# A two-layer decoder trunk: loading x from ScalarE's queue beside the weights, and a fixed order for the first three row tiles

## The chip, the cores and the metric

One core of a Trainium2 chip runs the whole program in one launch. The metric is device time in microseconds, the median of a few timed executions. The engines are TensorE (PE; its weight loads are listed as PEld), VectorE (DVE), ScalarE (ACT), GpSimd (POOL) and SyncE (SP, which here only issues DMAs). ScalarE can issue DMAs too; in the kernel before it issues none.

## The reference, cut to what matters

```python
def reference(x, ...):
    for l in range(DEPTH):                       # 2 layers
        h = _rmsnorm(x, pre_mix_norm[l])
        h = _hybrid_mixer(h, cos, sin, w_in[l], ...)   # proj = h @ w_in, then two kinds of mixing, then @ w_out
        x = x + _rmsnorm(h, post_mix_norm[l])
        h = _rmsnorm(x, pre_ffn_norm[l])
        h = _conv_glu_ffn(h, ffn_up[l], ...)
        x = x + _rmsnorm(h, post_ffn_norm[l])

def _rmsnorm(x, w):
    return (x * lax.rsqrt(jnp.mean(x * x, axis=-1, keepdims=True) + NORM_EPS)) * w
```

x is 512 positions by 1024 features, all in float32. The place of the change is the very first part: x times its gains, times the first columns of `w_in` (the keys of the DeltaNet heads) and times the eight small columns for `b` and `a` (the gates of these heads). The factor of the norm of each position (`rs` in the kernel) is multiplied in after the matmul.

## The kernel before, in words

**Three matmuls for one.** Each float32 operand is split into a high part in the matmul's own format and the rest: weights into `whi` and `wlo`, x times its gain into the two halves of `hx`. A product of a 128x128 piece of weights and a 128x512 piece of x is then a group of three matmuls: high by high, high by low, low by high (`mm3`, `mmk`). ScalarE writes the high part (`act`, L147), VectorE or GpSimd the low part (`tt`, L151; for x `stt`, L165), so a low part waits for its high part, and both for the landing of what they split.

**Row tiles.** x lies transposed: eight contraction tiles of 128 features by 512 positions, two to a tile `xt[0]` to `xt[3]`. A row tile is 128 columns of `w_in`: one unit of weights `raw`, 128x1024, for eight groups of three matmuls into one PSUM tile. The first three row tiles go to the three PSUM tiles `pss`, the later ones to `psg`. `was` are the split columns for `b` and `a`: 16 matmuls of 16 rows into a `psg`.

**The loads.** All DMAs go out on SP, in the order in which the program writes them: weight 0, the gains `vv`, x rows 0 and 1, weight 1, the three other pairs of x, `wa`, `rc`; then `loader` writes one load for every weight buffer that comes free. There are two `raw` buffers and four pairs of `whi` and `wlo` (HL).

**The order of the work.** The kernel's order is written by a planner in the program (`_Sched`): jobs are generators with priorities, a clock `sc.t` that adds up assumed costs, and flags with due times. The order in which jobs call an operation is the order of the instructions on its engine. `splitter` splits the weights in order, for the low part on VectorE or GpSimd, whichever the planner thinks free. `scale_split` splits an x tile; `square_sum` adds up x squared, with ScalarE squaring and GpSimd adding into `acc2`. `lead` multiplies whatever the planner takes for ready, row tile 0 first, then the `was` rows, then row tiles 1 and 2.

**What comes next.** From `acc2` four small matmuls, a step on VectorE (`rt`), a power on GpSimd and four more matmuls make `rs`, which ScalarE copies from PSUM. With it VectorE takes the row tiles out of PSUM (`A`), then works on the gates (`dn_...`), the convolution of the keys (`kT`) and the decays (`edec`). TensorE works on with further row tiles between them, in a fixed order in which rows that wait for VectorE stand.

**The warm-up.** Ahead of all this, five matmuls on a constant (`pso<-mhalf`) run while the loads are under way; each counts as two in the profile.

Of the kernel before, what the change touches and what calls it, by code (L numbers as in the profile page):

```python
# [10 lines left out]
F32 = mybir.dt.float32  # L11
# [7 lines left out]
P = 128  # L19
# [94 lines left out]
def kernel(ctx: ExitStack, tc: tile.TileContext, xT, w_ab, w_cm, w_tm, w_o, w_up, w_dn,  # L114
# [111 lines left out]
    for l in range(DEPTH):  # L226
# [10 lines left out]
        wseq += [(w_dn[l, m][:, 1024 * i:min(1024 * (i + 1), DFF)], min(1024, DFF - 1024 * i))  # L237
                 for m in range(KD) for i in range(3)]
        home[len(wseq) - 1] = ("xu", None)
    RAW, HL = 2, 4  # L240
    wraw, wunit = {}, {}
    wst = {"take": 0}

    def load(u, at):
        src, cols = wseq[u]
        raw = wp.tile([P, 1024], F32, tag="raw", bufs=RAW, name="raw")
        sync.dma_start(raw[:, :cols], src)
        wraw[u] = raw
        sc.set(("raw", u), at)

    def loader():
        sc.slots["raw"] = []
        for u in range(RAW, len(wseq)):
            yield from sc.get("raw", RAW)
            load(u, max(sc.t + 3.2, 13.4) if u == RAW else sc.t + 3.2)
            if u == RAW:
                sync.dma_start(cc, cst)

    def splitter():
        for u, (src, cols) in enumerate(wseq):  # L260
            yield from sc.wait(("raw", u))
            if u in home:
                tag, flag = home[u]
                if flag is not None:
                    yield from sc.wait(flag)
                if tag == "xu":
                    pair = xp.tile([P, 2, 768], F32R, tag="xu", name="wxu")
                else:
                    pair = sp.tile([P, 2, 1024], F32R, tag=tag, name="whome")
                hi, lo = pair[:, 0], pair[:, 1]  # L270
            else:
                yield from sc.get("wu", HL)
# [23 lines left out]
    def free(n=1, unit=None):  # L296
        for _ in range(n):
            if unit not in home:
                sc.put("wu", sc.t)
# [19 lines left out]
    def load_vec(l):  # L319
        v = cp.tile([P, V_W], F32, tag="vv", bufs=1, name="vv")  # L320
        sync.dma_start(v, vec[l])
        return v
# [15 lines left out]
        tt(was[:, :, 8:16], wa, was[:, :, 0:8].bitcast(F32), ALU.subtract, after=r)  # L338
        return was

    load(0, 4.0)
    vv = load_vec(0)
    for j in range(2):
        sync.dma_start(xt[0][:, j], xT[:, j])
    load(1, 7.3)
    for j in range(1, 4):
        sync.dma_start(xt[j], xT[:, 2 * j:2 * j + 2])
    wa0 = load_ab(0)
    rc = load_row(0)
    sc.set(("vec", 0))  # L350
# [27 lines left out]
    def scale_split(key, m, seg, hx, gain, acc2, after):  # L378

        t0, t1 = seg  # L380
        x = xs(m)[:, t0:t1]
        hi = hx[m][:, 0, t0:t1]
        r = act(hi, x, AF.Identity, scale=gain, after=after)
        if key != "in":
            sc.spawn(square_sum(key, m, seg, acc2), 0)
        yield r
        r = stt(hx[m][:, 1, t0:t1], x, gain, hi.bitcast(F32), ALU.mult, ALU.subtract, after=r)
        sc.set(("hx", key, m, t0), r)
        if key == "in":
            yield from sc.idle(("act",), 6.0)  # L390
            yield from square_sum(key, m, seg, acc2)

    def square_sum(key, m, seg, acc2):
        t0, t1 = seg
        x = xs(m)[:, t0:t1]
        if key != "in":
            yield from sc.wait(("rows", key, t0))
        if m == 0:
            r = act(acc2[:, t0:t1], x, AF.Square)
        else:  # L400
            sq = yield from wget("sq")
            r = act(sq[:, t0:t1], x, AF.Square)
            yield r
            yield from sc.wait(("sq", key, 0, t0))
            r = tt(acc2[:, t0:t1], acc2[:, t0:t1], sq[:, t0:t1], ALU.add, eng="pool", after=r)
            sc.put("sq", r)
        sc.set(("sq", key, m, t0), r)
# [245 lines left out]

    def mixer(l, key, hx, acc2, rs, segs):
        rhs = hl(hx)
        was = wab[l]
        pab = yield from pget("g")
        pss = []
        for _ in range(3):
# [4 lines left out]
        def ab_rows(kt, seg, first, last):  # L664
            t0, t1 = seg
            for j in range(2):
                mm(pab[0:16, t0:t1], was[:, kt], rhs(kt)[j][:, t0:t1], first and j == 0, last and j == 1)

        rt = kp.tile([P, 4], F32, tag="rt", bufs=1, name="rt")
        for seg in segs:  # L670
            yield from lead(key, pss, us, rhs, seg, seg is segs[-1], ab_rows)
            sc.spawn(pre_rstd(key, acc2, seg, rs, rt), 0)
        if l == 0:
            xd = xT
# [731 lines left out]
    def trunk():  # L1406
        nonlocal vv, rc
        key = "in"
        yield from sc.get("acc2", 1)
        acc2 = work("acc2")  # L1410
        yield from sc.get("rs", 1)
        rs = work("rs")
        hx = new_hx()
        tables(T_EXP)
        ps = yield from pget("o")
        for _ in range(5):
            mm(ps, mhalf[:, 0:1].to_broadcast([P, P]), mhalf[:, 0:1].to_broadcast([P, S]), True, True)
        pput("o", sc.t)
        for m in range(KD):
            sc.spawn(scale_split(key, m, FULL[0], hx, vv[:, V_PM + m:V_PM + m + 1], acc2, 0.0), 0,  # L1420
                     at=(5.2, 5.9, 8.9, 8.9, 10.3, 10.3, 11.8, 11.8)[m])
        def first_ab():
            yield 12.0
            wab[0] = yield from split_ab(wa0)
        sc.spawn(first_ab(), 0)
        while 0 not in wab:
            yield sc.t + 0.1
        for l in range(DEPTH):
            lx[0] = l
            mixt = yield from mixer(l, key, hx, acc2, rs, FULL if l == 0 else HALVES)  # L1430
            hx, acc2, rs = yield from out_rows((l, "m"), 3, hl(mixt), KD, V_QM, V_PF, None,
                                              flags=lambda k, l=l: (l, "mt", k))
            key = (l, "m")
            rhs, wait_hid = yield from ffn(key, hx, acc2, rs)
            if l + 1 < DEPTH:
                sc.spawn(next_ab(l + 1), 0)
            last = l == DEPTH - 1
            hx, acc2, rs = yield from out_rows((l, "f"), 1, rhs, KF, V_QF, None if last else V_NX, out, wait_hid)
            key = (l, "f")
            if not last:  # L1440
                sc.spawn(next_vec(l), 0)
# [107 lines left out]
```

## Time and the profile before

| | us |
|---|---|
| median of 3 executions | 1449.59 |
| lowest, highest | 1442.68, 1454.46 |
| the profiled execution | 1443.73 |
| its span | 1441.7 |
| TensorE busy | 1386.2 (96%) |
| VectorE busy | 940.9 (65%) |
| ScalarE busy | 613.0 (43%) |
| GpSimd busy | 566.6 (39%) |

Times in rows are microseconds from the start of the span. A row of the timeline holds start, duration, engine, line, operation, what is written from what, and how many instructions of the kind are merged in it; in square brackets stands how long the engine had been idle before it and who ended that. Most operations have a helper's line (L138 for every matmul), so rows are told apart by the tiles. In the rows for stages each engine has its busy time and count, then come TensorE's granted clock (1.00 is full), the share of the DMA engines and GB/s.

### The profile page before, as it was taken

How to read it: one execution, taken by the hardware profiler on the slowest of the kernel's cores; microseconds unless marked ns; L12 is line 12 of the kernel's file. 1: busy time of each engine (PE TensorE's matmuls, PEld its weight loads, DVE VectorE, ACT ScalarE, POOL GpSimd, SP SyncE). 2: the span in 40 equal slices, each digit the busy share in tenths (PEclk: the TensorE clock that was granted, in tenths of full speed). 3: DMA queues.
4: the chain of work that ended last, by engine and by line, in shares of the span. 5: the costliest groups of instructions: out<-in, count | busy, mean ns of one | idle time of the engine just before them, and what ended most of it. 6: DMA issues, size and time to landing. Idle time of an engine off the chain costs nothing. (4 is left out here: it accounts for less than half of the span.)

```text
span 1441.7 us, 18796 instructions
## 1 busy us (share of the span) xinstructions
PE 1386.2 (96%) x7174; PEld 1143.9 (79%) x7174; DVE 940.9 (65%) x1512; ACT 613.0 (43%) x992; POOL 566.6 (39%) x350
## 2 busy tenths in 40 slices
PE   8999999998999999999998999999989999999996
PEld 5778766878888888888886887668888888888886
DVE  4785467667598878831368844768586888787213
ACT  4453346445444443332245434565354444443220
POOL 3344255322444444423253541553143544443331
PEclk9999999999999999999999999999999999999998
DMA  5223211034133222333332331110422332223331
GB/s 197 74 90 86 61 30 45 16 117 132 44 90 101 88 88 89 96 120 95 113 115 73 94 98 30 44 45 16 146 89 69 93 101 89 88 88 106 110 91 59
DMA packets 48698, 123.15 MB, mean 85 GB/s; under 512 B 15584, under 2 KB 18400, under 8 KB 48608
## 3 DMA queue, kind: packets, MB, share of 16 engines
q1 hardware_dynamic: 48608, 121.95, 27.2%
q8 instruction: 57, 0.93, 0.3%
q14 instruction: 33, 0.27, 0.1%
HBM read 115.11 MB, written 6.82 MB: 85 GB/s over the span
## 5 line engine op out<-in xcount | busy, mean ns | idle before, releaser
L138 PE MATMUL psg<-hx,whi 128*128 128x512 f32 (+1 forms) x2080 | 631.1, 387 | 0.1
L151 POOL TENSOR_TENSOR wlo<-raw,whi 128x1024 fp32r<-128x1024 f32 (+1 forms) x142 | 355.6, 2515 | 510.3 <-ACT whi L147 490.5
L138 PEld LDWEIGHTS psg<-hx,whi 128*128 128x128 f32 x2080 | 379.7, 190 | 77.5 <-issue 4.4
L138 PE MATMUL psg<-hx,wlo 128*128 128x512 f32 (+1 forms) x1040 | 397.1, 382 | 0.0
L147 ACT ACTIVATE whi<-raw 128x1024 fp32r<-128x1024 f32 (+1 forms) x200 | 207.7, 1038 | 261.4 <-PE psg L138 196.5
L165 DVE SCALAR_TENSOR_TENSOR B<-A,vv,B 128x510 f32<-128x510 f32 (+1 forms) x176 | 265.6, 1511 | 70.2 <-ACT B L147 66.9
L138 PEld LDWEIGHTS psg<-hx,wlo 128*128 128x128 f32 x1040 | 197.1, 189 | 38.0
L138 PE MATMUL psg<-hid,whi 128*128 128x512 f32 (+1 forms) x744 | 213.4, 371 | 0.0
L138 PEld LDWEIGHTS psg<-hid,whi 128*128 128x128 f32 x744 | 135.7, 188 | 24.2
L151 DVE TENSOR_TENSOR wlo<-raw,whi 128x1024 fp32r<-128x1024 f32 (+1 forms) x58 | 75.7, 1307 | 111.7 <-ACT whi L147 111.5
L138 PE MATMUL psg<-hid,wlo 128*128 128x512 f32 (+1 forms) x372 | 137.9, 371 | 0.0
L138 PE MATMUL psg<-whi,hx 128*128 128x512 f32 x384 | 124.6, 406 | 0.3 <-DVE A L151 0.3
L151 POOL TENSOR_TENSOR acc<-acc,sq 128x256 f32<-128x256 f32 (+1 forms) x65 | 66.7, 1026 | 100.8 <-ACT sq L147 98.8
L147 ACT ACTIVATE hid<-C 128x512 fp32r<-128x512 f32 x44 | 27.8, 632 | 177.3 <-DVE C L151 177.3
L138 PEld LDWEIGHTS psg<-whi,hx 128*128 128x128 f32 x384 | 70.4, 192 | 13.7 <-DVE A L151 0.8
L138 PEld LDWEIGHTS psg<-hid,wlo 128*128 128x128 f32 x372 | 70.1, 188 | 11.9
L138 PE MATMUL psg<-wlo,hx 128*128 128x512 f32 x192 | 75.9, 395 | 0.0
L147 ACT ACTIVATE B<-A,vv 128x512 f32<-128x512 f32 x88 | 70.8, 809 | 7.0 <-DVE A L151 5.9
L151 DVE TENSOR_TENSOR A<-psg,rs 128x512 f32<-128x512 f32 x100 | 68.2, 684 | 2.0 <-POOL A L158 1.6
L147 ACT ACTIVATE C<-B 128x512 f32<-128x512 f32 x44 | 27.8, 632 | 71.3 <-DVE B L165 71.3
L138 PE MATMUL psg<-bT,bT 64*128 64x512 f32 (+3 forms) x128 | 48.1, 476 | 6.9 <-DVE nm L1196 4.2
L158 POOL TENSOR_SCALAR B<-B,den 128x512 f32<-128x512 f32 (+1 forms) x30 | 41.2, 1375 | 30.2 <-DVE den L177 17.4
(234 smaller groups left out, 1709.9 us busy)
## 6 DMA issues: line engine op xcount, KB each, us to landing
raw<-in_w_up_dram SPq DMA_DIRECT2D x88, 512.0 KB, 3.5
raw<-in_w_cm_dram SPq DMA_DIRECT2D x32, 512.0 KB, 3.6
raw<-in_w_dn_dram SPq DMA_DIRECT2D x32, 512.0 KB, 3.5
raw<-in_w_tm_dram SPq DMA_DIRECT2D x24, 512.0 KB, 3.5
raw<-in_w_o_dram SPq DMA_DIRECT2D x16, 512.0 KB, 3.6
raw<-in_w_dn_dram SPq DMA_DIRECT2D x16, 384.0 KB, 3.1
xt<-in_xT_dram SPq DMA_DIRECT2D x7, 512.0 KB, 6.9
scr_a<-am SPq DMA_DIRECT2D x8, 256.0 KB, 2.9
```

The source lines that it names most:

```text
L138: pe.matmul(ps, lhsT, rhs, start=start, stop=stop)
L147: nc.scalar.activation(out_, in_, func, **kw)
L151: (nc.vector if eng == "dve" else nc.gpsimd).tensor_tensor(out_, a, b, op=op)
L158: e.tensor_scalar(out_, a, s1, None, op0=op0)
L165: nc.vector.scalar_tensor_tensor(out_, a, s, b, op0=op0, op1=op1)
```

## The change

x is issued from ScalarE's queue, ahead of ScalarE's table load. Weight 0 is loaded in two halves, with the gains between them, and weight 2 right behind weight 1 into a buffer of its own (`s8`), so three weights are under way at the start. `opening` writes the splits of x and of the first three weights in one order by the table `FIRST` (kind, number, part, due time), all low parts on VectorE; the squares come behind them. `open_rows` writes the matmuls of the first three row tiles in one order, and the `was` rows behind them. The warm-up has three matmuls in place of five. The general `splitter` begins with weight 3.

```diff
-    RAW, HL = 2, 4
+    RAW, HL, OPEN = 2, 4, 3
...
     def load(u, at):
         src, cols = wseq[u]
-        raw = wp.tile([P, 1024], F32, tag="raw", bufs=RAW, name="raw")
-        sync.dma_start(raw[:, :cols], src)
+        if u == RAW:
+            raw = sp.tile([P, 2, 1024], F32, tag="s8", name="raw")[:, 0]
+        else:
+            raw = wp.tile([P, 1024], F32, tag="raw", bufs=RAW, name="raw")
+        parts = ((0, 512), (512, 1024)) if u == 0 else ((0, cols),)
+        for a, b in parts:
+            sync.dma_start(raw[:, a:b], src[:, a:b])
+            if u == 0 and a == 0:
+                sync.dma_start(vv, vec[0])
...
-    load(0, 4.0)
-    vv = load_vec(0)
+    vv = cp.tile([P, V_W], F32, tag="vv", bufs=1, name="vv")
     for j in range(2):
-        sync.dma_start(xt[0][:, j], xT[:, j])
-    load(1, 7.3)
-    for j in range(1, 4):
-        sync.dma_start(xt[j], xT[:, 2 * j:2 * j + 2])
+        for i in range(2):
+            nc.scalar.dma_start(xt[j][:, i], xT[:, 2 * j + i])
+    for j in range(2, 4):
+        nc.scalar.dma_start(xt[j], xT[:, 2 * j:2 * j + 2])
+    for u in range(OPEN):
+        load(u, 0.0)
...
+    FIRST = (("w", 0, 0, 4.0), ("x", 0, 0, 5.0), ("w", 0, 1, 5.0), ("x", 1, 0, 5.6), ("x", 2, 0, 6.4),
+             ("w", 1, None, 7.4), ("x", 3, 0, 8.2), ("x", 4, 0, 9.6), ("x", 5, 0, 9.6), ("w", 2, None, 10.0),
+             ("x", 6, 0, 11.2), ("x", 7, 0, 11.2))
+    def opening(hx, acc2):
+        for kind, i, part, at in FIRST:
+            if kind == "x":
+                yield from scale_split("in", i, FULL[0], hx, vv[:, V_PM + i:V_PM + i + 1], acc2, at)
+                continue
...
+            r = act(hi[:, cs], raw[:, cs], AF.Copy, after=at)
+            r = tt(lo[:, cs], raw[:, cs], hi[:, cs].bitcast(F32), ALU.subtract, after=r)
...
+        wab[0] = yield from split_ab(wa0)
+        for m in range(KD):
             yield from sc.idle(("act",), 6.0)
-            yield from square_sum(key, m, seg, acc2)
+            yield from square_sum("in", m, FULL[0], acc2)
+    def open_rows(pss, units, rhs):
+        order = [(0, 0), (0, 1), (0, 2), (1, 0), (1, 1), (1, 2)]
+        order += [(i, k) for k in range(3, 6) for i in range(2)] + [(2, k) for k in range(6)]
+        order += [(i, k) for k in range(6, 8) for i in range(3)]
+        for i, kt in order:
...
+            mmk(pss[i], unit, kt, rhs(kt), FULL[0], kt == 0, kt == KD - 1)
...
-            yield from lead(key, pss, us, rhs, seg, seg is segs[-1], ab_rows)
+            if key == "in":
+                yield from open_rows(pss, us, rhs)
+                for kt in range(KD):
+                    ab_rows(kt, seg, kt == 0, kt == KD - 1)
+            else:
+                yield from lead(key, pss, us, rhs, seg, seg is segs[-1], ab_rows)
...
-        for _ in range(5):
+        for _ in range(3):
             mm(ps, mhalf[:, 0:1].to_broadcast([P, P]), mhalf[:, 0:1].to_broadcast([P, S]), True, True)
...
+        sc.spawn(opening(hx, acc2), 0)
```

**ScalarE at the start of the program**, before. `xt_83` to `xt_86` are the four pairs of x, `hx_104` the split x.

```order
L219 ACT_TABLE_LOAD
L147 ACTIVATE whi<-raw 128x1024
L147 ACTIVATE hx_104<-xt_83,vv 128x512 x2
L147 ACTIVATE acc_102<-xt_83 128x512
L147 ACTIVATE sq<-xt_83 128x512
L147 ACTIVATE whi<-raw 128x1024
L147 ACTIVATE hx_104<-xt_84,vv 128x512 x2
```

And in the change, with what each row waits for. `DMAHW0` and so on are the semaphores of the transfers: 0 is that of x row 0, 2 that of x row 1, 1 that of the first half of weight 0, 3 that of the gains.

```order
L353 DMA xt_83<-in_xT_dram 128x512 x2
L353 DMA xt_84<-in_xT_dram 128x512 x2
L355 DMA xt_85<-in_xT_dram 128x1024 [waits DMAHW0_49]
L355 DMA xt_86<-in_xT_dram 128x1024 [waits DMAHW2_49]
L219 ACT_TABLE_LOAD
L147 ACTIVATE whi<-raw 128x512 [waits DMAHW1_49]
L147 ACTIVATE hx_108<-xt_83,vv 128x512 [waits DMAHW3_49]
L147 ACTIVATE whi<-raw 128x512 [waits DMAHW4_49]
L147 ACTIVATE hx_108<-xt_83,vv 128x512
L147 ACTIVATE hx_108<-xt_84,vv 128x512 [waits DMAHW5_49]
L147 ACTIVATE whi<-raw 128x1024 [waits DMAHW6_49]
```

Six DMA issues have moved in front of the table load, two of them waiting for transfers; a transfer's semaphore is used again by a later transfer, and the later issue waits for the earlier landing. The squares (`acc`, `sq`) have left the stretch.

**TensorE where it first waits for `edec`** (some 65 us into the kernel before), before. `hx_105` holds the contraction tiles 4 to 7, `pso<-cc,dn_g` are small rows for the decays, of which the second wait for VectorE's `edec`. Ahead of this piece stand seven row tiles and half of the eighth; the pair of rows in it comes three times.

```order
L138 MATMUL pso<-cc,dn_g 128x128 [waits PE_49]
L138 MATMUL pso<-cc,dn_g 128x128 x3
L138 MATMUL psg<-hx_105,whi 128x512 x2
L138 MATMUL psg<-hx_105,wlo 128x512
...
L138 MATMUL pso<-cc,dn_g 128x128 [waits DVE_49]
```

In the change eight whole row tiles stand ahead of the same rows, and the three groups between them belong to the next weights.

```order
L138 MATMUL pso<-cc,dn_g 128x128 [waits PE_49]
L138 MATMUL pso<-cc,dn_g 128x128 x3
L138 MATMUL psg<-whi,hx_108 128x512 [waits DVE_49,Activation_49]
L138 MATMUL psg<-whi,hx_108 128x512
L138 MATMUL psg<-wlo,hx_108 128x512 [waits Pool_49]
L138 MATMUL psg<-whi,hx_108 128x512 x2
L138 MATMUL psg<-wlo,hx_108 128x512
L138 MATMUL psg<-whi,hx_108 128x512 [waits DVE_49]
L138 MATMUL psg<-whi,hx_108 128x512
L138 MATMUL psg<-wlo,hx_108 128x512
L138 MATMUL pso<-cc,dn_g 128x128 [waits DVE_49]
```

So four groups of three matmuls have moved from behind the wait for `edec` to in front of it.

More of the change, by code (lines that the diff above doesn't have):

```diff
@@ L252, in loader @@
         sc.slots["raw"] = []
-        for u in range(RAW, len(wseq)):
+        for u in range(OPEN, len(wseq)):
             yield from sc.get("raw", RAW)
-            load(u, max(sc.t + 3.2, 13.4) if u == RAW else sc.t + 3.2)
-            if u == RAW:
+            load(u, max(sc.t + 3.2, 14.5 + 1.5 * (u - OPEN)) if u < OPEN + 2 else sc.t + 3.2)
+            if u == OPEN:
                 sync.dma_start(cc, cst)
     def splitter():
-        for u, (src, cols) in enumerate(wseq):
+        yield from sc.wait("open")
+        for u in range(OPEN, len(wseq)):
+            src, cols = wseq[u]
             yield from sc.wait(("raw", u))
@@ L385, in scale_split @@
             sc.spawn(square_sum(key, m, seg, acc2), 0)
-        yield r
+            yield r
         r = stt(hx[m][:, 1, t0:t1], x, gain, hi.bitcast(F32), ALU.mult, ALU.subtract, after=r)
         sc.set(("hx", key, m, t0), r)
-        if key == "in":
-            yield from sc.idle(("act",), 6.0)
-            yield from square_sum(key, m, seg, acc2)
+    FIRST = (("w", 0, 0, 4.0), ("x", 0, 0, 5.0), ("w", 0, 1, 5.0), ("x", 1, 0, 5.6), ("x", 2, 0, 6.4),
+             ("w", 1, None, 7.4), ("x", 3, 0, 8.2), ("x", 4, 0, 9.6), ("x", 5, 0, 9.6), ("w", 2, None, 10.0),
+             ("x", 6, 0, 11.2), ("x", 7, 0, 11.2))
@@ new lines, in opening @@
+    def opening(hx, acc2):
[3 more added lines that the diff above has]
+                continue
+            if not part:
+                yield from sc.get("wu", HL)
+                hi = wp.tile([P, 1024], F32R, tag="hi", bufs=HL, name="whi")
+                lo = wp.tile([P, 1024], F32R, tag="lo", bufs=HL, name="wlo")
+            raw = wraw[i]
+            cs = slice(0, 1024) if part is None else slice(512 * part, 512 * (part + 1))
+            r = act(hi[:, cs], raw[:, cs], AF.Copy, after=at)
+            r = tt(lo[:, cs], raw[:, cs], hi[:, cs].bitcast(F32), ALU.subtract, after=r)
+            if part != 0:
+                wunit[i] = (hi, lo)
+                wraw.pop(i)
+                sc.set(("wu", i), r)
+                if i < RAW:
+                    sc.put("raw", r)
+        sc.set("open", r)
+        wab[0] = yield from split_ab(wa0)
+        for m in range(KD):
+            yield from sc.idle(("act",), 6.0)
+            yield from square_sum("in", m, FULL[0], acc2)
@@ new lines, in open_rows @@
+    def open_rows(pss, units, rhs):
[3 more added lines that the diff above has]
+        for i, kt in order:
+            yield from sc.wait(("hx", "in", kt, 0))
+            unit = wunit.get(units[i])
+            while unit is None:
+                yield sc.t + 0.1
+                unit = wunit.get(units[i])
+            mmk(pss[i], unit, kt, rhs(kt), FULL[0], kt == 0, kt == KD - 1)
+            if kt == KD - 1:
+                wunit.pop(units[i])
+                free(unit=units[i])
+            yield
@@ L655, in mixer @@
         rhs = hl(hx)
-        was = wab[l]
         pab = yield from pget("g")
@@ L666, in ab_rows @@
             for j in range(2):
-                mm(pab[0:16, t0:t1], was[:, kt], rhs(kt)[j][:, t0:t1], first and j == 0, last and j == 1)
+                mm(pab[0:16, t0:t1], wab[l][:, kt], rhs(kt)[j][:, t0:t1], first and j == 0, last and j == 1)
         rt = kp.tile([P, 4], F32, tag="rt", bufs=1, name="rt")
         for seg in segs:
-            yield from lead(key, pss, us, rhs, seg, seg is segs[-1], ab_rows)
+            if key == "in":
[4 more added lines that the diff above has]
+                yield from lead(key, pss, us, rhs, seg, seg is segs[-1], ab_rows)
             sc.spawn(pre_rstd(key, acc2, seg, rs, rt), 0)
@@ L1415, in trunk @@
         ps = yield from pget("o")
-        for _ in range(5):
+        for _ in range(3):
             mm(ps, mhalf[:, 0:1].to_broadcast([P, P]), mhalf[:, 0:1].to_broadcast([P, S]), True, True)
         pput("o", sc.t)
[L1419 to L1427, printed above, removed]
+        sc.spawn(opening(hx, acc2), 0)
         for l in range(DEPTH):
```

## The prediction

> **What bounds the kernel now.** I read the busy shares first, then the 20 us stages for where TensorE is not busy, then the timeline of the first 35 us engine by engine. In a stage row the second number is TensorE's busy time.
>
> ```profile
> PE 1386.2 (96%) x7174; PEld 1143.9 (79%) x7174; DVE 940.9 (65%) x1512; ACT 613.0 (43%) x992; POOL 566.6 (39%) x350
> ...
> 0.00:20.00 20.00, 15.04 (x34) 7.81 (x34) 12.43 (x12) 13.68 (x20) 7.06 (x10) 0.91 0.66 235
> ...
> 60.00:80.00 20.00, 15.31 (x86) 12.84 (x85) 18.06 (x24) 14.28 (x19) 5.03 (x2) 0.94 0.16 50
> ```
>
> TensorE sets the time: 96% busy, so a gain is TensorE idle time that goes away and doesn't come back later. All idle time is 1441.7 - 1386.2 = 55.5 us; the first stage holds 5 us of it. The stage from 60 to 80 us loses almost as much, with VectorE 18 of 20 us busy: TensorE there waits for VectorE. So whatever the opening wins must also reach VectorE.
>
> The opening itself, TensorE's rows:
>
> ```profile
> 0.88 7.13 PE L138 MATMUL pso<-mhalf 128*128 128x512 f32 x10 [0.88 <-POOL mhalf L212]
> ...
> 7.45 1.03 PE L138 MATMUL pss<-hx,whi 128*128 128x512 f32 x2
> ...
> 20.07 3.88 PE L138 MATMUL psg<-hx,was 128*16 128x512 f32 x16 [1.48 <-DVE was L151]
> ...
> 23.56 0.42 PEld L138 LDWEIGHTS pss<-hx,whi 128*128 128x128 f32 x2
> ...
> 24.02 0.19 PEld L138 LDWEIGHTS pss<-hx,wlo 128*128 128x128 f32 x1
> ...
> 24.71 0.19 PEld L138 LDWEIGHTS pss<-hx,wlo 128*128 128x128 f32 x1
> ...
> 34.48 0.41 PEld L138 LDWEIGHTS psg<-hx,whi 128*128 128x128 f32 x2
> ```
>
> Three row tiles of eight contraction tiles are 24 groups of three matmuls. A group takes 24.71 - 24.02 = 0.69 us, so 16.6 us in all, and the `was` rows 23.56 - 20.07 = 3.5 us: 20.1 us. They end at 34.48, though the first starts at 7.45, when the warm-up ends: 7 us are lost. One tile alone is fed as x arrives, then `was` is waited for, and the other two tiles run only from 23.56.
>
> **The change, step by step.** The order rows shown with the change say that ScalarE issues six loads of x before its table load, the third waiting for the landing of x row 0 and the fourth for that of row 1. Does such an issue really hold its queue?
>
> ```profile
> SPq L257 <- DMA xt<-in_xT_dram: 0.3, 1, 0.3
> ...
> 7.46 0.33 SPq L257 DMA_DIRECT2D cc<-in_cst_dram  x1
> ...
> 0.72 1.28 ACT L219 ACT_TABLE_LOAD   x1 [0.72 <-PEq L1540]
> 4.44 1.06 ACT L147 ACTIVATE whi<-raw 128x1024 fp32r<-128x1024 f32 x1 [2.44 <-DMA raw<-in_w_cm_dram]
> 5.83 0.72 ACT L147 ACTIVATE hx<-xt,vv 128x512 fp32r<-128x512 f32 x1 [0.34 <-DMA xt<-in_xT_dram]
> 7.47 0.72 ACT L147 ACTIVATE hx<-xt,vv 128x512 fp32r<-128x512 f32 x1 [0.91 <-DMA xt<-in_xT_dram]
> ```
>
> It does on SP: `cc` was issued at 7.46, when x row 1 landed and ScalarE read it (7.47). On ScalarE the same wait holds everything behind it: the table load, hidden until now at 0.72, all splits, and through them VectorE and TensorE.
>
> *When x row 1 lands.* By bytes ahead on SP's queue, row 0 (512 + 132.5 + 256 = 900.5 KB) was read at 5.83 and row 1 (1156.5 KB) at 7.47. In the change row 1 has 512 KB on its own queue and, if the two queues share evenly, as much from SP: 1024 KB, so 5.83 + 1.64 x 123.5 / 256 = 6.6. Bounds: 4.44 (512 KB landed by then) and 7.47. I take 6.6.
>
> *ScalarE starts* after one more issue and the table load:
>
> ```profile
> 0.72 0.38 SPq L247 DMA_DIRECT2D raw<-in_w_cm_dram  x1
> ...
> 9.14 1.04 ACT L147 ACTIVATE whi<-raw 128x1024 fp32r<-128x1024 f32 x1
> ...
> 10.09 1.32 ACT L147 ACTIVATE hx<-xt,vv 128x512 fp32r<-128x512 f32 x2
> ...
> 5.53 1.23 DVE L151 TENSOR_TENSOR wlo<-raw,whi 128x1024 fp32r<-128x1024 f32 x1 [5.53 <-ACT whi L147]
> 6.67 0.74 DVE L165 SCALAR_TENSOR_TENSOR hx<-xt,vv,hx 128x512 fp32r<-128x512 f32 x1
> ```
>
> 6.6 + 0.4 + 1.28 = 8.3 us, against 4.44 now. An issue from ScalarE is not in the trace; SP's nearest rows give about 0.4, and a zero or a double moves the sum by 0.4. From 8.3 ScalarE no longer stops: 0.6 us for 512 columns (1.32 - 0.72), 0.95 for 1024 (10.09 - 9.14).
>
> VectorE follows at 8.9 with w0a, x0, w0b, x1, x2, w1: 0.62 + 0.74 + 0.62 + 0.74 + 0.74 + 1.23 = 4.7, done at 13.6 (ScalarE has w1 at 12.3). By then TensorE has three groups and two matmuls; 61 matmuls of 0.23 remain, 14.0 us, and the later splits stay ahead of it. End of the three tiles: 27.6. The last two loads of x, issued at 4.4 and 6.6 behind the same queue, are wanted at about 13.5 and 15.8, raw 2 before the latter; that cover is 2 us or more, and if it goes, it costs one for one.
>
> *The clock.* The last numbers of these rows are granted clock, share and GB/s:
>
> ```profile
> 12.00:14.00 2.00, 1.24 (x3) 0.48 (x3) 2.00 (x3) 2.00 (x4) 1.40 (x1) 0.73 1.02 401
> 14.00:16.00 2.00, 1.92 (x5) 1.55 (x6) 2.00 (x4) 1.99 (x4) 0.82 (x1) 0.50 0.60 245
> 16.00:18.00 2.00, 2.00 (x10) 1.63 (x9) 2.00 (x3) 1.90 (x3) 1.26 (x2) 0.92 0.00 0
> ```
>
> After sparse work TensorE had half its clock for (1 - 0.73) x 2 / 0.5 + 2.0 + 0.08 x 2 / 0.5 = 3.4 us, though the window before it still had 1.24 us of matmuls. In the change the three warm-up matmuls end near 6 (six rows at the first ones' pace of 0.855 us, 0.88 + 5.1), work starts near 9 and is sparse until 13.6. So a cold stretch can come again: 0 if it falls into the sparse part, 1.7 us if all of it is dense. I take 0.4, since sparse cold matmuls fill most of 9 to 13.6 and the clock may be back by then: 28.0. (The Trainium skill, "TensorE: Matmul & The Clock Gate", Part 1, has the clock fall only after an idle window of about 3.4 us. By it the gap of 3 us would cost nothing and the sum were 0.4 better. This trace has the clock fall without such a gap, so its rows are used.)
>
> With the `was` rows the opening ends at 31.5, against 34.48: **TensorE gains 3.0 us**. `was` itself, late now, is ready by 19:
>
> ```profile
> 17.24 2.69 POOL L151 TENSOR_TENSOR wlo<-raw,whi 128x1024 fp32r<-128x1024 f32 x1 [0.74 <-ACT whi L147]
> 17.64 2.38 DVE L151 TENSOR_TENSOR was<-wa,was 128x64 fp32r<-128x64 f32 x1
> ```
>
> Those 2.38 us for 64 columns ended with a GpSimd subtraction; the change has no GpSimd work there. It has the sums of squares later instead: the last two squares stand on ScalarE behind the splits of weights 4 and 5, which wait until TensorE frees units 0 and 1 (near 26.6 and 27.3), so they come by 30 and GpSimd's two additions by 33:
>
> ```profile
> 15.18 1.31 POOL L151 TENSOR_TENSOR acc<-acc,sq 128x512 f32<-128x512 f32 x1 [1.71 <-ACT sq L147]
> ```
>
> They are wanted at 36, seven groups into the fourth tile: 3 us of cover, then one for one. On SP raw 3 goes out when VectorE frees weight 0 near 11 and lands some 4 us later; it is wanted at 31.5. `xw` moves ahead of raw 6, which TensorE wants past 47. Both cost nothing.
>
> *What reaches VectorE.* Its long stretch starts with the row scale `rs`:
>
> ```profile
> 40.42 1.05 PE L138 MATMUL pso<-cc,rt 128*128 128x128 f32 x8
> 41.51 0.60 ACT L147 ACTIVATE rs<-pso 128x512 f32<-128x512 f32 x1 [5.77 <-PE pso L138]
> 42.14 1.29 DVE L151 TENSOR_TENSOR A<-pss,rs 128x512 f32<-128x512 f32 x2 [5.02 <-ACT rs L147]
> 45.90 0.17 DVE L158 TENSOR_SCALAR dn_beta<-dn_beta 128x16 f32<-128x16 f32 x1
> 49.25 8.84 DVE L165 SCALAR_TENSOR_TENSOR kT<-A,vv,kT 128x509 f32<-128x509 f32 x6
> ...
> 68.02 1.16 PE L138 MATMUL pso<-cc,dn_g 128*128 128x128 f32 x8 [2.36 <-DVE edec L151]
> ...
> 78.31 1.09 PE L143 MATMUL pss<-cc,kT 128*128 128x128 f32 x4 [1.70 <-DVE kd L151]
> ```
>
> In the change the rows that make `rs` stand 13 groups behind the opening (5 into the fifth tile): 13 x 0.69 + 0.7 for small rows = 9.7, then 42.14 - 40.42 = 1.7: `A` at 31.5 + 11.4 = 42.9, no earlier than now. But the gate rows ahead of `dn_beta` (43.4 to 45.9) have moved in front of `A`, so kT starts 1.29 + 3.35 later, at 47.5: 1.7 us earlier. The first wait for `edec` then ends at 66.3 instead of 68.02. TensorE gets there at 65.66 - 3.0 + 4 groups (2.8), that is 65.4, and waits 0.9. **Of 3.0 us 1.7 are left.**
>
> *Behind that* two more subtractions of `wlo` (1.23 each) move from GpSimd to VectorE ahead of the first `rab`:
>
> ```profile
> 94.41 1.12 DVE L165 SCALAR_TENSOR_TENSOR am<-pss,dn_br,edec 128x128 f32<-128x128 f32 x4 [1.03 <-PE pss L138]
> ...
> 96.67 1.12 DVE L165 SCALAR_TENSOR_TENSOR am<-pss,dn_br,edec 128x128 f32<-128x128 f32 x4 [1.06 <-PE pss L138]
> ...
> 103.78 0.63 PE L143 MATMUL pss<-cc,A 128*128 128x128 f32 x4 [0.16 <-DVE A L151]
> ...
> 252.85 2.07 PE L138 MATMUL psg<-bT,bT 64*128 64x512 f32 x2 [2.11 <-DVE nm L1196]
> ```
>
> VectorE idles 1.03 + 1.06 there, so 2.46 cost 0.4; bounds 0 and 2.5. I take 0.3. Until about 300 us the planner writes layer 0 in a slightly other order, from there on the same. Single waits up to 2.11 us lie in that stretch; a reshuffle can take or add one or two of them, so 0, bounds -3 and +3.
>
> **Sum:** -1.7 + 0.3 = -1.4 us. The profiled execution took 1443.73 (span 1441.7 and 2.0 around it), so 1442.3 on its scale; it lies 5.9 below the median 1449.59. The four known executions (1442.68, 1443.73, 1449.59, 1454.46) have the mean 1447.6; I count from it: **1446**.
>
> **Rivals.** *ScalarE isn't held* (the table load and splits run while the later x loads are in flight). For: the loads are short. Against: the `cc` row. Then raw 1 sets the pace: read at 9.14 now, w1 done on both engines near 11.3, the opening at 11.3 + 14.0 + 0.4 + 3.5 = 29.2, kT at 45.25: -4.0 + 0.3 = -3.7, so 1444.
>
> *The second queue brings nothing.* Transfers already fill the DMA engines (share 1.02 at 12 to 14 us), so row 1 lands at 7.47 as now; the hold ends 0.9 later and the gain is 0.5: 1447. (The Trainium skill, "DMA: Bandwidth & Descriptors", Issuing engines are not separate DMA queues, says that a second issuer saves only issuing time, which speaks for this.)
>
> *Slower: the hold takes more than the stall it removes.* Each us that x row 1 lands later than 6.6 costs one. It decides from 8.0. For: two weight tiles stream on SP's queue at that time. At the far end it lands with all eight first transfers (2180 KB; the same bytes were read by 10.09 now), 3.5 later: +2.1, 1450.
>
> *The table load is dearer there.* Rows inside the kernel speak against it:
>
> ```profile
> 68.19 1.28 ACT L219 ACT_TABLE_LOAD   x1
> 69.48 1.34 ACT L147 ACTIVATE vb<-A,vv 128x512 f32<-128x512 f32 x2
> ```
>
> The next instruction starts 0.01 us behind it. Were it double, the start moves by 1.3 and the gain is gone: 1448. (The Trainium skill, "ScalarE: Activation LUTs", What ACT_TABLE_LOAD costs, adds a drain of 1.38 us; these rows don't show it.)
>
> **How the numbers follow.** Forecast 0.45, not held 0.2, second queue nothing 0.15, slower 0.12, dearer table 0.03, a reshuffle in the attention of over 3 us 0.05. All cases lie within 1% (14 us, about what a measurement of this kernel can tell from no change); executions of one kernel alone spread over 12 us. So within 1%: 0.93, faster 0.04, slower 0.03. Range: lowest execution less 4, highest less 0.5: 1438 to 1454.
>
> **What would show it.** ScalarE's table load near 7 us and first split near 8.3; TensorE idle between 6 and 9 us, dense from 13.6; `was` rows ending near 31.5; `rs` near 42; the wait for `edec` below 1.5 us; from 300 us the same rows, 2 us earlier. A table load before 3 us, or a first split before 6, makes the forecast wrong.

## The result, and the profile after

The change takes 1452.74 us in the median of 20 executions (1445.32 to 1464.49), the kernel before 1442.44 us (20 executions, 1438.06 to 1457.20). The ratio is 1.006, with a 95% interval of 1.0038 to 1.0082: slower by 0.6%. The time lies inside the forecast range (1438 to 1454), but on the other side of the kernel before: 0.1% faster was forecast. The profiled execution of the change took 1464.49 us (span 1462.7), the slowest of its twenty; that of before took 1443.73, near the median. So the two profiles differ by twice what the medians do.

The opening went as worked out. The share line of the page of the change:

```profile
PE 1406.8 (96%) x7170; PEld 1159.4 (79%) x7170; DVE 937.6 (64%) x1517; ACT 613.0 (42%) x992; POOL 558.1 (38%) x347
```

and ScalarE and TensorE in the timeline of its first 36 us (start, duration, engine, operation, idle time and its releaser in brackets):

```profile
6.33 1.28 ACT L219 ACT_TABLE_LOAD   x1 [6.33 <-DMA xt<-in_xT_dram]
7.62 0.63 ACT L147 ACTIVATE whi<-raw 128x512 fp32r<-128x512 f32 x1
...
8.92 0.50 PE L138 MATMUL pss<-hx,whi 128*128 128x512 f32 x1 [2.54 <-ACT hx L147]
...
31.19 0.41 PEld L138 LDWEIGHTS psg<-hx,whi 128*128 128x128 f32 x2
```

The loads of x do hold ScalarE's queue, the first split starts at 7.62 (8.3 forecast), and the fourth row tile starts at 31.19 in place of 34.48: 3.3 us earlier. What is new stands further on. The 20 us stages of the block inversion in layer 0, first of the change, then of before (stage, then busy time of each engine, then granted clock, share and GB/s):

```profile
140.00:160.00 20.00, 18.51 (x111) 15.21 (x110) 9.46 (x17) 3.56 (x5) 7.39 (x4) 0.84 0.39 105
160.00:180.00 20.00, 20.00 (x100) 16.13 (x99) 4.38 (x15) 4.15 (x8) 0.00 (x0) 0.50 0.00 1
```

```profile
140.00:160.00 20.00, 19.38 (x126) 15.45 (x125) 9.60 (x20) 4.13 (x6) 5.58 (x4) 0.91 0.35 90
160.00:180.00 20.00, 20.00 (x157) 15.26 (x157) 9.33 (x34) 10.06 (x24) 3.71 (x3) 1.00 0.09 27
```

From 160 to 180 us TensorE is busy all the time in both, but at clock 0.50 in the change, and gets 100 matmul records done where before has 157. In the block inversion TensorE runs batches of mostly 8 or 16 small matmuls (64x16 to 128x128) between single groups of large ones. The clock falls there in both kernels; before it comes back after 3.4 us, in this execution of the change it stays down for 27 us. In layer 1 it stays down for 24 us from 874 us, against 6.8 us before.

Most of the loss goes with the granted clock. Time at half clock, (1 - clock) x 2 x span, is 58 us in the profile of before (clock 0.98) and 105 us in that of the change (0.964). A straight line through 20 executions of the change gives 1448.8 us at clock 0.975, one through 35 executions of before 1450.0: at the same clock the kernels differ by less than 0.1%. About 12 us hang on 0.01 of clock. (With the twelve executions of the change's second run, less one that stands off the line at clock 0.922 and 1458.86 us, the change has 1449.4.)

Where the two kernels part in layer 0 is one wait. `xi` holds the inverse of the DeltaNet heads' triangular matrices, which is built up from blocks. These are the second group of four transposes of `xi` in the change, and the engines behind it:

```profile
151.84 0.42 DVE L151 TENSOR_TENSOR xi<-C,cc 128x256 f32<-128x256 f32 x1
152.42 2.36 POOL L151 TENSOR_TENSOR wlo<-raw,whi 128x1024 fp32r<-128x1024 f32 x1 [4.40 <-PE pss L138]
...
152.81 2.25 DVE L151 TENSOR_TENSOR xi<-C,cc 128x256 f32<-128x256 f32 x1
...
153.12 0.60 PE L1024 MATMUL pss<-cc,xi 128*64 128x128 f32 x4
...
155.20 1.03 PE L1024 MATMUL pss<-cc,xi 128*64 128x128 f32 x4 [1.49 <-DVE xi L151]
```

and the same place of before:

```profile
150.65 2.36 POOL L151 TENSOR_TENSOR wlo<-raw,whi 128x1024 fp32r<-128x1024 f32 x1 [4.64 <-ACT whi L147]
...
151.38 1.92 DVE L151 TENSOR_TENSOR xi<-C,cc 128x256 f32<-128x256 f32 x1
...
153.44 1.89 PE L966 MATMUL pss<-cc,xi 128*64 128x128 f32 x8 [0.62 <-DVE xi L151]
153.59 0.43 DVE L151 TENSOR_TENSOR xi<-C,cc 128x256 f32<-128x256 f32 x1
```

VectorE expands two chunks of `xi` one after the other, 0.42 us each. A GpSimd split of a weight (2.36 us) runs beside one of them, and that one takes 1.9 to 2.25 us: it ends 0.28 us behind GpSimd (152.42 + 2.36 = 154.78, 152.81 + 2.25 = 155.06). Before, the split hits the first expansion. The change's new row order puts the weight split 1.77 us later (152.42 against 150.65) but the expansions only 0.46 later (151.84 against 151.38), and so the split hits the second. TensorE has done the first four transposes by then and waits 1.49 us for the other four. (The Trainium skill, "SBUF — State Buffer", SBUF: two separate sides, says that VectorE with two SBUF inputs and GpSimd lock one port pair for a whole instruction, and the other blocks. The rows agree: 0.42 us alone, 2.25 behind GpSimd.)

The wait doesn't make the clock fall here. In the change's profile the clock is at half from 153.59 us, while the first four transposes still run; the wait begins at 153.72 (153.12 + 0.60). Before, it falls at 152.85. What the wait can do is keep it from coming back.

In layer 1 this profile has no such wait, though it has a long stretch: the split hits the first expansion there, as it does in the kernel before, and TensorE waits 0.41 us.

```profile
873.13 2.36 POOL L151 TENSOR_TENSOR wlo<-raw,whi 128x1024 fp32r<-128x1024 f32 x1 [5.52 <-ACT whi L147]
873.39 2.38 DVE L151 TENSOR_TENSOR xi<-C,cc 128x256 f32<-128x256 f32 x1
...
875.91 1.89 PE L1024 MATMUL pss<-cc,xi 128*64 128x128 f32 x8 [0.41 <-DVE xi L151]
```

So the wait in layer 0 is a suspect, which the experiments below try.

### The profile page after: what moved, and what is told of

Its sections match the earlier page's. It is cut to its first block, busy times and chain, and to the rows that moved or that the text cites. A ratio compares the mean times of both kernels' runs of the same rounds, so it can differ in the third digit from the quotient of the medians.

```text
span 1462.7 us, 18800 instructions
## 1 busy us (share of the span) xinstructions
PE 1406.8 (96%) x7170; PEld 1159.4 (79%) x7170; DVE 937.6 (64%) x1517; ACT 613.0 (42%) x992; POOL 558.1 (38%) x347
## 5 line engine op out<-in xcount | busy, mean ns | idle before, releaser
L151 POOL TENSOR_TENSOR wlo<-raw,whi 128x1024 fp32r<-128x1024 f32 (+1 forms) x138 | 345.3, 2512 | 521.8 <-ACT whi L147 498.8
L147 ACT ACTIVATE whi<-raw 128x1024 fp32r<-128x1024 f32 (+2 forms) x201 | 207.7, 1034 | 263.1 <-PE psg L138 197.6
L151 DVE TENSOR_TENSOR wlo<-raw,whi 128x1024 fp32r<-128x1024 f32 (+2 forms) x63 | 79.7, 1269 | 117.3 <-ACT whi L147 117.2
L138 PE MATMUL psg<-whi,hx 128*128 128x512 f32 x384 | 130.1, 422 | 2.4 <-DVE A L151 2.4
L138 PE MATMUL psg<-bT,bT 64*128 64x128 f32 (+3 forms) x128 | 48.4, 477 | 3.5 <-DVE nm L1254 2.1
L138 PE MATMUL pss<-hx,whome 128*128 128x256 f32 x288 | 43.7, 308 | 5.9 <-DVE hx L165 5.3
```

Source lines behind the costliest of these rows:

```text
L138: pe.matmul(ps, lhsT, rhs, start=start, stop=stop)
L147: nc.scalar.activation(out_, in_, func, **kw)
L151: (nc.vector if eng == "dve" else nc.gpsimd).tensor_tensor(out_, a, b, op=op)
```

## The experiments

Ratios are to the kernel before, run on the same chip. Where executions are counted below 1448 us, from there to 1459 and above, it is because they stand in groups some 10 us apart.

### First: order or opening?

The change and the kernel before were run again, and the change with a delay in its plan. With 3.0 the matmuls behind the opening stand in the order of before, but for one group of three; with 6.0 the rows that make `rs` stand further ahead:

```diff
                 yield from open_rows(pss, us, rhs)
+                yield sc.t + 3.0      # 6.0 in a second version
```

> The changed kernel once more, to see how its granted clock and its time go together over several executions. In the first profile of the change the opening ends at 31.2 us (forecast 31.5), so the opening is not what is slow; TensorE's half-clock stretches add up to 92 us against 55 us before. Theory A (clock): executions differ by the granted clock alone, about 0.5 us of time for each us at half clock; this profile again has more than 70 us at half clock, and the stretch from 150 to 180 us is again at half clock for longer than 10 us. Theory B (the rows in another order cost TensorE busy or idle time at any clock): the time stays over 1.005 of before even where the half-clock time is that of before. Theory C (that profile was only an unlucky one): half-clock time near 55 us here and a ratio near 1.000.

> The kernel before as a run of its own, for its clock and a second profile: ratio 1.000 within the interval. Theory A: half-clock time 50 to 65 us, granted clock 0.978 to 0.982 in most executions, and its slower executions have the lower clock. Theory B: the clock of before and of the change are alike on average.

> The new opening, with 3.0 us of the planner's own time let pass between the opening and what follows: from the fourth row tile on the rows then stand as before the change. One line. Theory A and the forecast's sum: the opening's 3 us are kept as far as VectorE allows and the half-clock stretches return to those of before (50 to 65 us in all): ratio 0.996 to 1.000. Theory A': order of the rows doesn't matter for the clock, the shorter warm-up or the shifted start does: ratio 1.004 to 1.008, clock 0.972 as in the change. Theory B with the opening as the cause: 1.004 to 1.008 too, at an unchanged clock.

> The same with 6.0 us: the rows that make rs stand four groups further ahead (3 groups behind the sums of squares instead of 6), so VectorE's stretch should start some 2 to 3 us earlier than in the run with 3.0. If VectorE sets the waits between 60 and 80 us, as the forecast has it, TensorE's waits there shrink: ratio 0.994 to 0.998, rs by 39 us. If the clock alone decides: like the run with 3.0, within 0.002 of it. If the sums of squares come too late for that place, TensorE waits there for GpSimd for 1 us or more and nothing is won.

| kernel | median us | ratio, interval |
|---|---|---|
| the change again | 1454.11 | 1.0062 (1.003 to 1.0093) |
| before again | 1443.60 | 1.0003 (0.9973 to 1.0034) |
| old order (3.0) | 1444.24 | 0.9995 (0.9962 to 1.0027) |
| 6.0 | 1442.23 | 0.9972 (0.9941 to 1.0003) |

The loss repeats, and it goes with the order behind the opening, not with the opening. One thing that was expected of the second run of the change didn't come: its profile (1457.69 us) has only 6.8 us at half clock in layer 0, and the clock is back at 160 us.

```profile
156.20:159.60 3.40, 3.40 (x28) 2.62 (x28) 1.57 (x8) 0.69 (x1) 0.00 (x0) 0.70 0.25 101
159.60:163.00 3.40, 3.40 (x44) 2.68 (x43) 1.89 (x7) 1.58 (x4) 0.00 (x0) 1.00 0.02 5
```

The split hits the second expansion there too, but the clock had fallen earlier, at 151.39, so that TensorE was slower at its first transposes and waited only 0.20 us. The long stretch of that execution, 24 us, is in layer 1. The second profile of before (1452.73 us) has one of 20.5 us in layer 1 as well. So the overlap makes a long stretch likely, not certain.

The opening by itself brings nothing that can be measured, though its fourth tile starts 2.9 us earlier than before's here too. The old order's profile shows a reason, in TensorE's timeline and in the 4 us stages around it:

```profile
33.96 1.13 PE L138 MATMUL pso<-cc,acc 128*128 128x1 f32 x8 [1.33 <-POOL acc L151]
```

```profile
32.00:36.00 4.00, 2.67 (x14) 2.04 (x13) 0.75 (x2) 1.06 (x1) 3.83 (x3) 0.85 0.59 187
36.00:40.00 4.00, 4.00 (x14) 3.18 (x13) 0.00 (x0) 0.00 (x0) 1.33 (x2) 0.72 0.45 131
```

The rows behind the sums of squares wait 1.33 us for GpSimd, and the clock falls to 0.72, where before has neither. With 6.0 that wait is 1.34 us; the ratio is in the expected range (0.994 to 0.998), but its interval just includes 1.

### Second: the overlap taken away, or the wait filled

In two kernels the two splits (weight unit 22 in layer 0, unit 126 in layer 1) go to VectorE behind the second expansion; every other instruction keeps its place on its engine:

```diff
+            if u in (22, 126):
+                yield from sc.wait(("expand", u // 100))      # set behind the second expansion
+                nc.vector.tensor_tensor(lo[:, :cols], raw[:, :cols], hi[:, :cols].bitcast(F32), op=ALU.subtract)
```

In the third a matmul of a constant stands ahead of the transposes that wait:

```diff
             ps = yield from pget("s")
+            if c < 2:
+                pe.matmul(ps, mhalf[:, 0:1].to_broadcast([P, P]), mhalf[:, 0:1].to_broadcast([P, S]), start=True, stop=True)
```

The fourth is the old order with the table load ahead of the loads of x, and five constant matmuls at the start in place of three.

> The change with one instruction per layer moved from GpSimd to VectorE: the lo part of weight unit 22 (layer 0) and of unit 126 (layer 1), 2.36 us on GpSimd, which in the traces runs at the same time as one of the first two expansions of xi in the block inversion (0.42 us on VectorE alone, 1.8 to 2.4 us beside it). The rest of the order stays. Theory A (TensorE waits for xi because of this overlap, the clock falls in that wait and may stay at half for over 20 us through the small matmuls; more so in the change's order): the expansion takes 0.43 us in both layers, the wait for xi is gone, the stretch at half clock near 152 to 182 us and near 870 to 898 us is gone or 3.4 us, mean granted clock 0.98 or higher, time 1443 us or less against the change's 1453, ratio to before 1.000 or less. Rival B (the clock falls because of the small matmuls themselves): clock as in the change, 0.972, ratio 1.006. Rival C (the loss is in other waits that the order makes): less than 3 us come back.

> The kernel before with the same two instructions moved from GpSimd to VectorE. Theory A: it gains too, but less than the change does, since it has 3.4 us at half clock there in layer 0 and either 7 or 21 us in layer 1: 2 to 5 us less, ratio 0.997 to 0.999. Rival B: ratio 1.000. If the 1.23 us that VectorE then takes are waited for: 1.001 to 1.002.

> The change with a matmul of a constant (two instructions of 0.43 us at full clock; its result is overwritten) ahead of the first two groups of transposes of xi in each layer, which is where TensorE waits up to 1.5 us; the overlap of GpSimd and VectorE stays, and with it the late xi. It adds 3.4 us of TensorE work in all, most of it inside the wait. Theory A with the clock as the carrier: the half clock in those two places shrinks to 3.4 us or nothing, mean clock 0.98, time 1445 to 1448 us. If the wait's own length costs and not the clock: no gain, 1453 to 1456 us.

> The kernel that has the change's opening and the order of before behind it (ratio 0.9995 earlier), with two edits in the opening: the table load of ScalarE ahead of the loads of x on its queue, and five matmuls of a constant at the start as in the kernel before in place of three. Theory: the hold of ScalarE by its loads and the table load behind them (6.33 to 7.61 us) set the first split; with the table load first the first split starts near 6.4 us in place of 7.6, the row tiles' first matmul near 7.7 in place of 9.0, and TensorE has no idle stretch of 3.4 us ahead of it, so that the half clock before 16 us goes from 6.8 to 3.4 us or less: 1.3 + 1.4 = 2.7 us less, ratio 0.9977. Rival (the rows of x landing set the dense start, near 10 us, in any case): ratio 0.999 to 1.000.

| kernel | median us | ratio, interval |
|---|---|---|
| change, splits on VectorE | 1442.50 | 1.001 (0.9983 to 1.0037) |
| before, splits on VectorE | 1441.59 | 1.0006 (0.9974 to 1.0037) |
| change, wait filled | 1454.57 | 1.0056 (1.0016 to 1.0096) |
| old order, table load first | 1441.57 | 0.9985 (0.9954 to 1.0016) |

Two moved instructions give back the whole loss. The profile of the first has both expansions at 0.42 us and the split behind them:

```profile
151.66 0.42 DVE L151 TENSOR_TENSOR xi<-C,cc 128x256 f32<-128x256 f32 x1
...
153.15 0.42 DVE L151 TENSOR_TENSOR xi<-C,cc 128x256 f32<-128x256 f32 x1
153.49 1.22 DVE L296 TENSOR_TENSOR wlo<-raw,whi 128x1024 fp32r<-128x1024 f32 x1
...
154.10 1.91 PE L1031 MATMUL pss<-cc,xi 128*64 128x128 f32 x8
```

Two expectations failed. The kernel before gained nothing from the same move, and its profile (1450.05 us) has a stretch of 27.3 us at half clock in layer 0, from 172.9 us, with the overlap gone and TensorE busy all the time from 160 us on (stages of 4 us, as above):

```profile
168.00:172.00 4.00, 4.00 (x29) 2.59 (x28) 3.15 (x13) 0.49 (x2) 1.80 (x1) 1.00 0.28 65
172.00:176.00 4.00, 4.00 (x23) 2.93 (x22) 2.19 (x9) 3.00 (x9) 0.61 (x1) 0.61 0.18 71
176.00:180.00 4.00, 4.00 (x18) 2.57 (x16) 0.51 (x4) 0.78 (x2) 0.92 (x1) 0.50 0.00 0
```

And filling the wait didn't help: the time came out where the rival had it (1453 to 1456 us: the wait's own length costs). But in that profile the half clock at the filled wait in layer 0 does last only 3.4 us, as the theory had it; a stretch of 27.3 us stands instead from 894 us, later in the inversion of layer 1. 8 of its 12 executions took over 1454 us. So neither theory holds there as it stands: it isn't only the idle TensorE that counts, and with the wait filled, the second transposes stand even later (157.03 us against 155.20).

The old order with the table load first has its first split at 6.42 us in place of 7.70 and `was` rows from 25.77 in place of 28.12; the first small matmuls of the inversion, at 146.81 against 149.19, still have that. In time it lies between theory (0.9977) and rival (0.999 to 1.000), and the interval holds both.

### Third: the same cause put into the kernel before

A GpSimd instruction of 0.2 us that reads an expansion holds the split, on GpSimd, until that expansion is done. Behind the first expansion (in before) the split always hits the second; behind the second (in the change) it hits none. No other instruction moves.

```diff
             r = expand(xi[:, c, :, lo], y, 32, C_BD + 8, after=r)
+            if c == 0:      # in before; c == 1 in the change
+                nc.gpsimd.tensor_tensor(probe, xi[:, c, 0, 0:16], xi[:, c, 0, 0:16], op=ALU.mult)
```

Two more kernels add the edits up: the delay of 6.0, and the change's own order, both with the table load first, five constant matmuls and the splits on VectorE.

> The kernel before, with a tiny GpSimd instruction that reads the first expansion of xi put ahead of the split of weight units 22 and 126, so that the 2.36 us split starts behind the first expansion and always lies beside the second (as in the change's trace of layer 0); every other instruction keeps its place. Theory A (the place of the overlap decides: on the second expansion TensorE waits 1.5 us and the clock stays at half for 20 us and more): the wait for xi is 1.5 us in both layers, mean clock 0.972, time 1450 to 1454 us, ratio 1.005 to 1.007. Rival B (the long stretches at half clock are a draw of the whole order, and the overlap only one part of it): under 3 us more, ratio 1.000 to 1.002, though the wait is there.

> The change, with the same tiny GpSimd instruction reading the second expansion, so that the splits of units 22 and 126 stay on GpSimd but start behind both expansions. Nothing else moves, and VectorE gets no work more. Theory A: as with the split on VectorE: no wait for xi, 1442 to 1444 us, ratio 0.999 to 1.002, mean clock 0.979. Rival B: anything between 1442 and 1456, most likely like the change's 1453, ratio 1.005 to 1.007.

> The version of the change with the later rows held back by 6 us in the plan (ratio 0.997 earlier), with the table load ahead of the loads of x, five matmuls of a constant at the start, and the splits of units 22 and 126 on VectorE behind the expansions. Theory A: the parts add: 2 us from the opening, the overlap's stretches gone: 1437 to 1440 us, ratio 0.995 to 0.997. Rival B: 1441 to 1443, ratio 0.998 to 1.000.

> The change in its own order, with the three edits (table load first, five matmuls at the start, the two splits on VectorE behind the expansions). Theory A: 1442.5 us as with the splits alone, less up to 2 us by the opening: 1440 to 1442, ratio 0.998 to 0.9995. Rival B: the opening shifts the windows in which the clock is set, and the long stretches come back: 1446 to 1452, ratio 1.002 to 1.006.

| kernel | median us | ratio, interval |
|---|---|---|
| before, split on the second expansion (6 executions) | 1463.65 | 1.0118 (1.0076 to 1.0161) |
| change, split behind both | 1444.89 | 0.999 (0.9959 to 1.002) |
| 6.0 and all edits | 1437.65 | 0.9974 (0.9947 to 1.0001) |
| change and all edits | 1441.46 | 0.9982 (0.9954 to 1.001) |

The profile of the first, layer 0, shows the change's picture in the kernel before, in the timeline and in the stage behind it:

```profile
151.14 2.36 POOL L151 TENSOR_TENSOR wlo<-raw,whi 128x1024 fp32r<-128x1024 f32 x1
151.42 2.35 DVE L151 TENSOR_TENSOR xi<-C,cc 128x256 f32<-128x256 f32 x1
...
153.92 1.03 PE L972 MATMUL pss<-cc,xi 128*64 128x128 f32 x4 [1.59 <-DVE xi L151]
```

```profile
160.00:180.00 20.00, 20.00 (x100) 16.16 (x99) 3.75 (x12) 5.33 (x10) 0.61 (x1) 0.50 0.00 1
```

An instruction of 0.2 us, twice, made the kernel before some 17 us slower. That is about twice the change's loss and more than was expected (1450 to 1454 us). In its profile both layers have a long stretch, 27.3 and 20.5 us. With the split held behind both, the change has 12 of 12 executions below 1448 us; as it was written, 7 of 32.

### Fourth: which layer?

> The change, with the GpSimd split held behind both expansions in layer 0 alone (unit 22); layer 1 as it was. Theory A0 (the change's loss is the place of the overlap in layer 0): nearly all of it returns, 1443 to 1447 us, ratio 1.000 to 1.002, no execution above 1459. Rival A1 (the loss comes from layer 1, whose moment has shifted): 1450 to 1454, ratio 1.004 to 1.007.

> The change, with the GpSimd split held behind both expansions in layer 1 alone (unit 126). Theory A0: less returns than with layer 0: 1448 to 1453 us, ratio 1.003 to 1.006. Rival A1: 1443 to 1447, ratio 1.000 to 1.002. If both layers count alike, h1 and h2 each give back half: 1447 to 1449.

> The kernel before, with the split held behind the first expansion in layer 0 alone, so that the overlap lies on the second expansion there, as in the change. Theory A0: the change's loss without the change: about 1452 us, ratio 1.005 to 1.007. If one long stretch at half clock costs 10 us and layer 1 keeps its own draw: a group near 1450 and a group near 1462. Rival: under 3 us.

> The kernel before, with the splits of both layers held behind both expansions, on GpSimd. Theory A: its executions above 1448 us (13 of 35) go, 1440 to 1442 us, ratio 0.997 to 0.999. If the overlap on the first expansion costs nothing and the long stretches of before come from elsewhere: as before, ratio 1.000, a third of the executions above 1448.

| kernel | median us | ratio, interval | below 1448, to 1459, above |
|---|---|---|---|
| change, held in layer 0 only | 1445.51 | 1.0021 (1.0004 to 1.0039) | 10, 2, 0 of 12 |
| change, held in layer 1 only | 1459.96 | 1.0119 (1.0078 to 1.016) | 1, 2, 3 of 6 |
| before, second hit in layer 0 only | 1449.21 | 1.009 (1.0056 to 1.0124) | 0, 5, 4 of 9 |
| before, held in both layers | 1440.12 | 0.9983 (0.9966 to 1.0) | 12, 0, 0 of 12 |

Layer 0 is the change's own loss: held there, most of it returns; held in layer 1 only, none does (1459.96 us where 1448 to 1453 was expected; six executions, and a wide interval). The same fault in layer 0 of before alone makes two groups near 1449 and 1462 us, as expected if layer 1 goes its own way. The last line points to before paying too, in its slower executions: with both layers held, none of 12 is above 1448. But on that chip only 4 of 26 executions of before were (48 of 157 over all chips), so chance is not ruled out.

The eighteen profiles, one execution each, say how far the place of the overlap decides. Each has two places, one in each layer. A stretch of 20 us or more at half clock begins within 4 us of the first expansion in 8 of 12 places where the split hits the second expansion, in 2 of 10 where it hits the first, and in none of 14 where it hits neither. In all six places where TensorE waits 1.2 us or more for the second transposes, the stretch is a long one. Two more long stretches begin elsewhere in the inversion, at 172.9 us in the kernel before with its splits on VectorE, and at 894 us in the change with the wait filled. So the place of the overlap in layer 0 is what costs the change its time, but it isn't the only thing that can hold the clock down.

## Why the prediction was right and wrong

*The opening: right.* The queue is held, the table load starts at 6.33 (near 7 forecast), the first split is 0.7 us earlier than forecast, TensorE gains 3.3 us (3.0). The rival that ScalarE isn't held is refuted. So are the second queue that brings nothing and the hold that takes longer, since x row 1 had landed by 6.33 (6.6 taken, 7.47 without a gain), and the dearer table load: the next instruction starts 0.01 us behind it. The clock term (0.4 taken, 0 to 1.7 possible) was of the right kind: one stretch of 3.4 us at half clock between 8 and 16 us in this profile, though 6.8 us in the second one.

*What reaches VectorE: right as far as kT, then less.* Forecast was `A` at 42.9, `kT` at 47.5, and 1.7 of 3.0 us kept. The timeline of the change, VectorE and GpSimd, then TensorE:

```profile
43.43 1.29 DVE L151 TENSOR_TENSOR A<-pss,rs 128x512 f32<-128x512 f32 x2 [2.31 <-ACT rs L147]
...
45.84 2.40 POOL L151 TENSOR_TENSOR wlo<-raw,whi 128x1024 fp32r<-128x1024 f32 x1 [6.87 <-ACT whi L147]
45.86 2.42 DVE L158 TENSOR_SCALAR dn_t<-dn_t 128x16 f32<-128x16 f32 x1
...
50.16 6.56 DVE L165 SCALAR_TENSOR_TENSOR kT<-A,vv,kT 128x509 f32<-128x509 f32 x6
...
66.51 0.68 DVE L151 TENSOR_TENSOR edec<-pso,dn_gc 128x512 f32<-128x512 f32 x1
...
58.27 0.73 PE L138 MATMUL psg<-hx,whi 128*128 128x512 f32 x2 [2.04 <-DVE A L151]
...
75.21 2.08 PE L138 MATMUL pso<-cc,dn_g 128*128 128x128 f32 x8 [2.95 <-DVE edec L151]
77.53 1.09 PE L143 MATMUL pss<-cc,kT 128*128 128x128 f32 x4 [0.25 <-DVE kd L151]
```

and of before:

```profile
47.19 0.17 DVE L158 TENSOR_SCALAR dn_t<-dn_t 128x16 f32<-128x16 f32 x1
...
67.28 0.68 DVE L151 TENSOR_TENSOR edec<-pso,dn_gc 128x512 f32<-128x512 f32 x1
```

`kT` started at 50.16, 2.7 us late, since one VectorE instruction on 16 columns took 2.42 us in place of 0.17 beside a GpSimd split that started 0.02 us ahead of it. But its six instructions end at 56.72 against 58.09, 1.4 us earlier: before, it was `kT` that a split stretched (8.84 us against 6.56; the split started at 49.21, 0.04 us ahead of `kT`). So the sum held there, by two errors that cancel. Behind it the gain runs out: 0.8 us at the first `edec` (66.51 against 67.28). TensorE, which is early, waits for VectorE's `A` (2.04 us) and for a later `edec` (2.95, where below 1.5 was expected), and from 75 us it has half its clock for 10.2 us, against 3.4 us before: 6.8 us more, worth up to 3.4 us. The forecast has no term for that. At the transposes of `kT` the change is 0.8 us ahead (77.53 against 78.31), at the first small matmuls of the inversion 0.46 behind (149.39 against 148.93).

*The step that failed* is the one on the rows behind: "a reshuffle can take or add one or two of them, so 0, bounds -3 and +3". I priced the reshuffle by TensorE's single waits, which are up to 2.11 us. The wait that it added in layer 0 is of that size (1.49 us), but the half clock around it is not: up to 27 us in place of 3.4; half of the difference is 12 us, by an estimate, and the groups of executions stand some 10 us apart. The term was set at 0 with 3 us to either side, and the loss is about 10 us in the median. The rows that could have said so were in the profile of before: an expansion of 1.92 us followed by one of 0.43, under a GpSimd split. And the clock was weighed in the opening alone, though 58 us of the span ran at half clock. Why the clock stays down after such a wait is open. The rival "a reshuffle in the attention of over 3 us" had a chance of 0.05; its sign was left open, and it named no mechanism.

*The range: luck.* That 1452.74 lies inside 1438 to 1454 owes to the width, which came from the spread of four executions. The forecast also counted from their mean, 1447.6, and the median of twenty turned out at 1442.44. Less 1.4 us that is 1441.0, and the change took 11.7 us more.

*From 300 us the same rows, 2 us earlier:* the rows are the same, but in this profile some 9 us later, and 21 us at the end. With the overlap held off in both layers the change stands at 0.999 of before, which is what the sum of -1.4 us would make; but the interval (0.9959 to 1.002) holds no gain as well, and with the splits on VectorE the ratio was 1.001. So the gain forecast behind the opening is not shown.

## What to carry to other kernels

When an edit shifts the order of work, look for short VectorE instructions on the critical path that lie beside long GpSimd ones: which of two neighbours is hit can be worth more than the edit. A wait ahead of a stretch of small matmuls can cost more than its length (here 1.5 us and some 10 us), since the clock may not come back for over 20 us; so ask of each wait what TensorE runs behind it. And when executions of one kernel stand in groups, compare the groups and their clocks before explaining the median.

## What the runs showed of the hardware

- TensorE stayed at half clock with no idle time in the profile: 20.00 us busy of 20 at 0.50 (the stage from 160 us). Its clock also fell with no idle time ahead, at 172.9 us in the kernel before with its splits on VectorE (4.00 us busy of 4 in the rows shown). Stretches at half clock last about 3.4, 6.8, 10.2, 20.5, 23.9 or 27.3 us in these profiles, steps of 3.4, apart from the last of each profile. (The Trainium skill, "TensorE: Matmul & The Clock Gate", Part 1, has the clock set by a free-running window of 3.4 us; the steps agree. It has one busy window bring the clock back; by the profile's own busy time the stage at 160 us doesn't show that.) What in the small matmuls keeps the clock down was not tried.
- Why filling the wait moved a long stretch to a later place instead of removing it stays open.
- VectorE's 128x16 instruction of 0.17 us took 2.42 beside GpSimd, and its 128x256 instruction of 0.42 us took 2.25; both ended within 0.3 us of GpSimd's end. So the delay goes by what is left of the GpSimd instruction, not by the size of VectorE's.
- The fastest version, all edits with the delay of 6.0, took 1437.65 us in the median, with an interval of the ratio that just includes 1 (0.9947 to 1.0001).
